# Reordering the seams of a two-layer hybrid attention block: the merge starts with its own loads, one projection moves ahead of the compressed keys, and the memory norm's transposes are emitted later

## The chip, the cores and the metric

The kernel runs on one core of one Trainium2 chip. Times are microseconds (us) on the device, for one execution of the whole program; the time shown is the median of three runs.

## What is computed

Two layers of a block on 1024 tokens of width 1024, in float32, with a memory of 256 rows. Cut to what matters here:

```python
def hybrid_layer(x, mem, ...):
    h = rms_norm(x, g_pre)
    parts = jnp.split(h @ w_in, IN_SPLITS, axis=-1)
    y_a = chunked_gmlp(a_u, a_v, ...) * silu(a_z)                  # branch 0
    y_b = nsa_attention(b_q, b_kc, b_vc, ...) * silu(b_z)          # branch 1
    y_c = forgetting_attention(c_q, c_k, c_v, ...) * silu(c_z)     # branch 2
    y_m = memory_attention(m_q, mem, g_mem, ...) * silu(m_z)       # branch 3
    up = einsum('bsnw,nwd->bsnd', stack([y_a, y_b, y_c, y_m]), w_br)
    gates = sigmoid(einsum('bsd,dne->bsne', h, w_gate))
    out = einsum('bsnd,bsnd->bsd', gates, up) @ w_o
    return x + rms_norm(out, g_post)

def memory_attention(q, mem, g_mem, w_mem_kv):
    mk, mv = split(rms_norm(mem, g_mem) @ w_mem_kv, 2)             # keys and values of the memory
    ...
def nsa_attention(...):
    kcmp, vcmp = compress(kc, ...), compress(vc, ...)              # silu(blocks @ w1) @ w2
    ...
```

## The kernel before, in words

**Arithmetic.** Every float32 operand of a large product is split into a high part and a low part (`split`: ScalarE copies the high part, VectorE or GpSimd subtracts it), and each product is three matmuls (`mm3`, lines 251, 254 and 255): high x high, high x low, low x high. One projection of 128 columns over all 1024 tokens (`proj`, twice) is 48 matmuls of 128x512. Weights are loaded by `weight` (DMA, then ScalarE and GpSimd split them) into rings of 2 or 3 tiles.

**Order.** The kernel emits its instructions in program order, and a planner (`schedule_with_timeline_sim=True`) then orders them for each engine by emission order and by its own model of time, over the whole program: an instruction that is ready may be placed before earlier ones that are not. `hot()` gives what is emitted inside it precedence over everything outside. `pace`/`follow`/`mark` add orderings between matmuls: each score matmul of the attention is a mark, and a paced projection's matmul k is tied behind a mark that lies proportionally far along. `order_slots` at the end adds one more rule: the tiles of one pool are first written in program order, so the first write of a tile waits for the first write of the tile allocated before it in its pool. All DMAs of the program are issued from one queue, SP's.

**Pools that matter here.** `st` is a ring of eight 128x512 tiles for everything short-lived (projection results, loads of y, gate results). `pp` is a ring of twelve 128x512 score tiles, open from `gates` to the end of `attention`. `yh` (five tiles of 128x4x512) opens in `merge`, after `pp` is closed, over the same memory, and waits tile by tile for what lay there. While `early` is True (in `gates` and until `fox` begins), two of three tiles asked of `st` come from `pp` instead, and projections take banks of two PSUM pools.

**A layer.** `gates` computes the gmlp branch's inputs, values, and some merge gates. `attention` (line 1255) runs `cmp_proj` (rope and split of the compressed branch's inputs, stored to `kcd` and `vcd`), `fox` (which begins with `compress`, the products of `kcd`/`vcd` at line 897, then four pairs of heads), `nsa_proj`, four `mem_proj` (queries of the memory attention, each 48 matmuls and four stores to `mqd`), and `nsa` with the memory units. Projections that come later in the program serve as filler between the score products. After the units, `FILL` lists paced filler: gmlp parts, early gates and `gate_out` (silu of a z projection, times the attention's output `od`, stored to `y`). Its last item is y4, an early gate.

**The merge.** In `merge` (line 1277) the first thing is `gate_out(1, "bz", 3)`, the one gate that needs the last heads of the nsa branch: for each half c it asks for tiles z and oo, loads oo from `od` (line 1215), computes z (tanh at line 341, product at 342), multiplies on GpSimd (1217) and stores y (1218). Then `add_branch(n)` for n = 0, 2, 3, 1 loads that branch's y (`get_y`, line 1316: eight loads), splits it into yh and yl (lines 331 and 335) and, for eight column blocks e and two token halves c, multiplies by w_br (twelve matmuls), loads or computes the gate th (line 1325) and accumulates (line 1332 for n = 0). Branch 0's y is written by the gmlp parts and does not need the last heads. Then `out_proj(0)`, `mem_norm` of the next layer (hot), `out_proj(1)`, and the next layer's `mem_kv` and `prenorm`. `norm_t` (line 377) loads a tile, scales it and at once turns it by transposes on TensorE (line 396) and splits it. `out_proj(c)` is two products of 96 matmuls (line 301), q = 0 and 1, each closed by squares on ScalarE (line 1359).

Of the kernel before, what the change touches and what calls it, by code (L numbers as in the profile page):

```python
# [19 lines left out]
F32 = mybir.dt.float32  # L20
# [193 lines left out]
class Net:  # L214
# [159 lines left out]
        nc.gpsimd.tensor_tensor(r, ms, self.mhalf, op=OP.pow)  # L374
        return r

    def norm_t(self, src, g, n_t, put):

        nc = self.nc
        for i in range(n_t):  # L380
            x = self.pvv.tile([128, 1024], F32, name="x", tag="slot")
            nc.sync.dma_start(x, src[i * 128:(i + 1) * 128, :])
            if i == 0:
                gb = self.ptp.tile([128, 2, 512], F32, name="gb", tag="pt2")
                nc.sync.dma_start(gb, g.rearrange("(q c) -> q c", q=2).partition_broadcast(128))
            r = self.rstd(x, EPS, i % 2 == 1)
            for q in range(2):
                xq = x[:, q * 512:q * 512 + 512]
                if q:
                    nc.scalar.activation(xq, xq, AF.Copy, scale=r)  # L390
                    nc.gpsimd.tensor_mul(xq, xq, gb[:, q])
                else:
                    nc.vector.scalar_tensor_tensor(xq, xq, r, gb[:, q], op0=OP.mult, op1=OP.mult)
                pt = self.ppt.tile([128, 4, 128], F32, name="pt")
                for k in range(4):
                    nc.tensor.transpose(pt[:, k, :], xq[:, k * 128:(k + 1) * 128], self.ident)
                hi, lo = put(i, q)
                self.split(hi, lo, pt)


    def layer(self, l):
# [709 lines left out]
            nc.sync.dma_start(self.y[0][g, :, cs], u)  # L1111


    def mem_norm(self, l):
        a = self.a
        mt = [[self.pkk.tile([128, 4, 256], R32, name="mt", tag="slot") for _ in range(2)] for _ in range(2)]
        def put(i, q):
            s = (slice(None), slice(None), slice(i * 128, i * 128 + 128))
            return mt[0][q][s], mt[1][q][s]
        with self.hot():  # L1120
            self.norm_t(a["mem"], a["g_mem"][l], 2, put)
        self.mt = mt

    def mem_kv(self):

        nc, mt = self.nc, self.mt
        m = lambda y, k: mt[y][k // 4][:, k % 4, :]
        for h in range(4):
            hi, lo = self.a_form(f"mk{h}")
            ps = self.pj()  # L1130
            self.mm3(ps[:, :256], [(hi[:, k, :], lo[:, k, :], m(0, k), m(1, k)) for k in range(8)])
            t = self.st("mk", R32)
            with self.hot():
                self.split(t[:, :256], t[:, 256:], ps[:, :256])
            self.move(self.mkd[h], t)
        for n in range(2):
            hi, lo = self.b_form(f"mv{n}")
            for i in range(2):
                ps = self.pj()
                sl = slice(i * 128, i * 128 + 128)  # L1140
                self.mm3(ps[:, :256], [(m(0, k)[:, sl], m(1, k)[:, sl], hi(k), lo(k)) for k in range(8)])
                t = self.st("mv", R32)
                with self.hot():
                    self.split(t[:, :256], t[:, 256:], ps[:, :256])
                for x in range(2):
                    v = t.rearrange("p (y h d) -> p y h d", y=2, h=2)[:, :, x, :]
                    self.move(self.mvd[2 * n + x, :, i], v)
# [60 lines left out]
    def gate_out(self, n, name, p):  # L1208
# [3 lines left out]
        for c in range(2):  # L1212
# [4 lines left out]
            nc.gpsimd.tensor_mul(z, z, o)  # L1217
            nc.sync.dma_start(self.y[n][p, :, cs], z)

    def gate_early(self, n, e):  # L1220

        w = self.a_form(f"g{n}{e}")
        for c in range(2):
            t = self.st("th")
            self.gate_store(n, e, c, t, self.proj(w, c))
# [28 lines left out]

    def attention(self):
        self.cmp_proj()
        self.fox()
        self.nsa_proj()
        for h in range(4):
            self.mem_proj(h)  # L1260
        self.todo = [(7 * h + 3 + 3 * c, lambda h=h, c=c: self.mem_unit(h, c)) for h in range(4) for c in range(2)]
        self.step, self.marks = 0, []
        self.nsa()
        names = FILL.split()
        self.pace = (0, sum(4 if n[0] == "u" else 2 for n in names) * 24 // (3 * STEP), STEP, SLACK)
        for name in names:
            h = int(name[1])
            if name[0] == "u":
                self.gmlp_u(h)
            elif name[0] in "wy":  # L1270
                self.gate_early({"w": 0, "y": 2}[name[0]], h)
            else:
                self.gate_out(*{"c": (2, "cz"), "m": (3, "mz"), "b": (1, "bz")}[name[0]], h)
        self.pace = None


    def merge(self):
        nc, tc, a, l = self.nc, self.tc, self.a, self.l
        p = lambda n, b: tc.tile_pool(name=n, bufs=b, reuse_waits="tile")
        with p("yh", 5) as self.pyh:  # L1280
            with p("acc", 1) as pacc:
                self.acc = [pacc.tile([128, 8, 512], F32, name=f"acc{c}") for c in range(2)]
                self.gate_out(1, "bz", 3)
                for n in (0, 2, 3, 1):
                    self.add_branch(n)
            gp = self.pyh.tile([128, 1024], F32, name="gp", tag="yh")
            nc.sync.dma_start(gp, a["g_post"][l].partition_broadcast(128))
            self.early = "banks"
            with p("kf", 4) as self.pkk, p("vf", 3) as self.pvv, p("tf", 1) as self.ptp:
                self.out_proj(0, gp)  # L1290
                if l + 1 < self.depth:
                    self.mem_norm(l + 1)
                self.out_proj(1, gp)
                if l + 1 < self.depth:
                    self.l, self.xsrc = l + 1, self.x1
                    self.fresh()
                    self.mem_kv()
                    self.prenorm()

    def add_branch(self, n):  # L1300
        yy = [self.get_y(n, c) for c in range(2)]
        for cs in ((0, 1),) if n != 1 else ((0,), (1,)):
            for e in range(8):
                wg = None if (n, e, 0) in self.ready else self.a_form(f"g{n}{e}")
                if e % 2 == 0:
                    wu = [z.rearrange("p (e w c) -> p e w c", e=2, w=4) for z in self.weight(f"u{n}{e // 2}")]
                for c in cs:
                    self.gated(n, e, c, wg, [z[:, e % 2] for z in wu], yy[c])
# [35 lines left out]
                for x in self.fin.pop(c):  # L1344
                    self.split(*x)

    def out_proj(self, c, gp):

        nc = self.nc
        hi, lo = self.mh[c]  # L1350
        ot = [self.pyh.tile([128, 2, 1024], F32, name="ot", tag="yh") for _ in range(2)]
        ss = [self.psm.tile([128, 2], F32, name="oss") for _ in range(4)]
        for q in range(2):
            qs = slice(q * 512, q * 512 + 512)
            def done(i, ps):
                sq = self.pcs.tile([128, 512], F32, name="sq", tag=("co", "si")[i % 2])
                with self.hot():
                    nc.vector.tensor_mul(ot[i // 2][:, i % 2, qs], ps, gp[:, qs])
                    nc.scalar.activation(sq, ps, AF.Square, accum_out=ss[i][:, q:q + 1])
            self.proj_wide(f"wo{q}", hi, lo, done, tail=c == q == 1)  # L1360
        for i in range(4):
            t0 = c * 512 + i * 128
            ms = self.psm.tile([128, 1], F32, name="oms")
            r = self.psm.tile([128, 1], F32, name="ors")
            with self.hot():
                nc.vector.reduce_sum(ms, ss[i], axis=AX.X)
                nc.vector.tensor_scalar(ms, ms, 1.0 / D, 4 * EPS, op0=OP.mult, op1=OP.add)
                nc.gpsimd.tensor_tensor(r, ms, self.mhalf, op=OP.pow)
            for x in range(2):
                xs = slice(x * 512, x * 512 + 512)  # L1370
                xr = self.st("xr")
                nc.sync.dma_start(xr, self.xsrc[t0:t0 + 128, xs])
                with self.hot():
                    nc.vector.scalar_tensor_tensor(xr, ot[i // 2][:, i % 2, xs], r, xr, op0=OP.mult, op1=OP.add)
                    nc.sync.dma_start(self.xdst[t0:t0 + 128, xs], xr)
# [87 lines left out]
```

## Time and profile before

| | us |
|---|---|
| median of 3 runs | 3156.19 (3148.03 to 3160.84) |
| the profiled execution's own time | 3157.73 |
| its span, first to last instruction | 3155.9 |
| TensorE busy | 3047.0 (97%) |
| VectorE, ScalarE, GpSimd busy | 1884.3, 1487.9, 1439.2 |
| mean granted TensorE clock | 0.989 of full |

A busy TensorE is one with a matmul under way; the idle time in brackets behind a row of the timeline is the time in which that engine stood still just before, and the name behind the arrow is what ended it. Layer 0 runs from 0 to about 1500, layer 1 from there to the end.

### The profile page before, as it was taken

Reading aid. Unit: us, or ns where it says so; the run is one execution under the profiler, and the core shown is the slowest. Engines: PE = TensorE matmul, PEld = TensorE weight load, DVE = VectorE, ACT = ScalarE, POOL = GpSimd, SP = SyncE. Lnnn points to the kernel's source line nnn. Section 1 sums busy time; section 2 is a strip of 40 time slices with the busy share of each in tenths; the row PEclk is TensorE's granted clock in tenths of the full one; section 3 lists DMA queues with packets and bytes.
Section 4 is the critical chain, followed back from the end, with each engine's and each line's share of the span. In section 5 each row is a group of like instructions: output and inputs, shape, how many; then the busy total and the mean of one; then the engine's idle time right before and its main releaser. Section 6 shows DMA issues by size and latency. Waiting matters only on the chain.

```text
span 3155.9 us, 45143 instructions
## 1 busy us (share of the span) xinstructions
PE 3047.0 (97%) x15168; PEld 2548.8 (81%) x15168; DVE 1884.3 (60%) x4313; ACT 1487.9 (47%) x3313; POOL 1439.2 (46%) x1142
## 2 busy tenths in 40 slices
PE   7999999999999999899999999999999999998998
PEld 6778878888888888688787788788878888886887
DVE  7555447868667855336474653578785678553363
ACT  5433345566556654323353433455655566552132
POOL 6844534543233322258577445355432333232684
PEclk9999999999999999999999999999999999998999
DMA  6544495564234322456665345855632342324564
GB/s 221 153 134 132 140 276 158 177 191 125 84 108 146 106 94 94 139 174 195 205 201 177 104 130 162 251 164 180 200 104 83 113 146 96 105 89 149 171 197 147
DMA packets 251673, 475.15 MB, mean 151 GB/s; under 512 B 42513, under 2 KB 96785, under 8 KB 251441
## 3 DMA queue, kind: packets, MB, share of 16 engines
q1 hardware_dynamic: 251440, 472.26, 47.6%
q8 instruction: 120, 1.97, 0.3%
q14 instruction: 113, 0.92, 0.1%
HBM read 334.73 MB, written 137.43 MB: 150 GB/s over the span
## 4 chain that ended last, share of the span: by engine, by line
PE 82%; DVE 5%; DMA 4%; POOL 3%; issue 2%; ACT 2%; SPq 1%; DVEq 0%; POOLq 0%; ACTq 0%
PE pj L251 11%; PE pj L254 11%; PE pj L255 11%; PE s L481 5%; PE s L301 5%; PE s L254 5%; PE o L645 5%; PE s L251 5%; PE s L255 5%; PE pt L633 5%; PE pj L481 4%; PE pj L301 4%; PE s L601 3%; PE s L602 3%; DVE p L674 1%
## 5 line engine op out<-in xcount | busy, mean ns | idle before, releaser
L229 POOL TENSOR_TENSOR wl<-wr,wh 128x1024 fp32r<-128x1024 f32 (+1 forms) x232 | 527.4, 2275 | 609.9 <-ACT wh L227 535.0
L251 PE MATMUL pj<-hh,wh 128*128 128x512 f32 x1648 | 651.5, 395 | 2.4 <-DVE z L342 1.8
L255 PE MATMUL pj<-hh,wl 128*128 128x512 f32 x1648 | 652.3, 396 | 0.0
L254 PE MATMUL pj<-hl,wh 128*128 128x512 f32 x1648 | 650.5, 395 | 0.0
L227 ACT ACTIVATE wh<-wr 128x1024 fp32r<-128x1024 f32 x232 | 245.5, 1058 | 341.1 <-PE s L254 86.7
L611 ACT ACTIVATE p<-p,nm 128x384 f32<-128x384 f32 (+3 forms) x512 | 306.8, 601 | 203.5 <-DVE nm L606 200.4
L333 DVE TENSOR_TENSOR pt<-pt,pt 128x512 fp32r<-128x512 f32 (+1 forms) x464 | 291.9, 635 | 134.8 <-ACT pt L331 133.4
L251 PEld LDWEIGHTS pj<-hh,wh 128*128 128x128 f32 x1648 | 310.9, 189 | 61.0 <-DVE z L342 2.7
L255 PEld LDWEIGHTS pj<-hh,wl 128*128 128x128 f32 x1648 | 310.6, 188 | 59.2
L254 PEld LDWEIGHTS pj<-hl,wh 128*128 128x128 f32 x1648 | 310.6, 188 | 58.0
L331 ACT ACTIVATE pt<-pt 128x512 fp32r<-128x512 f32 (+1 forms) x464 | 251.7, 554 | 212.5 <-PE pt L633 154.3
L645 PE MATMUL o<-pt,v 128*128 128x512 f32 (+1 forms) x864 | 245.1, 371 | 8.8 <-DVE pt L333 8.5
L654 POOL TENSOR_TENSOR yt<-yt 128x256 f32<-128x256 f32 x128 | 100.1, 782 | 300.9 <-ACT yt L653 241.0
L633 PE MATMUL pt<-ident,p 128*128 128x128 f32 x1488 | 230.6, 272 | 0.7 <-DVE pt L333 0.5
L251 PE MATMUL s<-yh,wh 128*128 128x512 f32 x512 | 201.1, 396 | 24.7 <-ACT yh L331 24.7
L633 PEld LDWEIGHTS pt<-ident,p 128*128 128x128 f32 x1488 | 184.9, 140 | 43.0 <-DVE pt L333 0.7
L254 PE MATMUL s<-yl,wh 128*128 128x512 f32 x512 | 201.4, 393 | 0.8 <-DVE yl L335 0.8
L255 PE MATMUL s<-yh,wl 128*128 128x512 f32 x512 | 200.7, 392 | 0.0
L601 PE MATMUL s<-kd,q 128*128 128x512 f32 (+2 forms) x512 | 187.4, 369 | 13.2 <-DVE nm L606 13.2
L602 PE MATMUL s<-kl,q 128*128 128x512 f32 (+2 forms) x512 | 175.5, 344 | 0.0
L645 PEld LDWEIGHTS o<-pt,v 128*128 128x128 f32 x864 | 147.6, 188 | 33.4 <-DVE pt L333 13.6
L676 DVE TENSOR_SCALAR p<-p,r,sg 128x384 f32<-128x384 f32 (+2 forms) x320 | 165.9, 574 | 1.7
(379 smaller groups left out, 6577.4 us busy)
## 6 DMA issues: line engine op xcount, KB each, us to landing
wr<-wt SPq DMA_DIRECT2D x250, 512.0 KB
th<-thd SPq DMA_DIRECT2D x124, 256.0 KB
thd<-gu SPq DMA_DIRECT2D x72, 256.0 KB
q<-rq SPq DMA_DIRECT2D x32, 512.0 KB
yf<-y SPq DMA_DIRECT2D x64, 256.0 KB
thd<-th SPq DMA_DIRECT2D x52, 256.0 KB
vd<-vs SPq DMA_DIRECT2D x48, 256.0 KB
v<-vd SPq DMA_DIRECT2D x24, 512.0 KB
```

What stands on the lines that cost most here:

```text
L229: nc.gpsimd.tensor_sub(lo[:, :n], raw[:, :n], hi.bitcast(F32)[:, :n])
L251: ins = nc.tensor.matmul(out, ah, bh, start=k == 0, stop=False)
L254: nc.tensor.matmul(out, ah, bl, start=False, stop=False)
L255: nc.tensor.matmul(out, al, bh, start=False, stop=k == n - 1)
L301: self.nc.tensor.matmul(ps[i], a[:, kk, ts], b[:, k], start=kk == n == 0, stop=kk == 7 and n == 2)
L333: (nc.gpsimd if pool else nc.vector).tensor_sub(lo, src, hi.bitcast(F32))
L481: nc.tensor.matmul(out, w[a][:, k], t[b][:, k], start=start and k == x == 0, stop=k == 3 and x == 2, skip_group_check=True)
L601: self.mark(nc.tensor.matmul(ps[:, :w], q[:, tq], kd[:, b0:b0 + w], start=True, stop=False), 1 + n / 128)
L602: nc.tensor.matmul(ps[:, :w], q[:, tq], kl[:, b0:b0 + w], start=False, stop=True)
L611: nc.scalar.activation(p[:, :n], p[:, :n], AF.Exp, bias=init, scale=-1.0, accum_out=l[:, x:x + 1])
L633: nc.tensor.transpose(pt[:, off + x * 128:off + x * 128 + 128], src, self.ident)
L645: nc.tensor.matmul(o[:, :, t0:t0 + m], it["v"], w[:, :, off:off + m], start=first, stop=last)
```

## The change

Three edits. (1) The merge no longer begins with `gate_out(1, "bz", 3)`. `add_branch(0)` asks for its eight loads of y first, then begins the gate (`gate_begin`: both projections and both silus, the matmuls tied behind the last score product), and finishes it (`gate_end`: loads of oo, multiplications, stores of y) when column block e = 2 comes up. (2) `mem_proj(0)` is emitted between `cmp_proj` and `fox`, so ahead of `compress`, while `early` is still True. (3) `mem_norm` of the next layer returns its transposes and splits unmade, and `out_proj(1)` emits them, hot, after its first product.

```diff
-    def norm_t(self, src, g, n_t, put):
+    def norm_t(self, src, g, n_t, put, later=False):
+        nc, rest = self.nc, []
+        def turn(xq, i, q):
+            pt = self.ppt.tile([128, 4, 128], F32, name="pt")
+            for k in range(4):
+                nc.tensor.transpose(pt[:, k, :], xq[:, k * 128:(k + 1) * 128], self.ident)
+            hi, lo = put(i, q)
+            self.split(hi, lo, pt)
...
-                pt = self.ppt.tile([128, 4, 128], F32, name="pt")
-                for k in range(4):
-                    nc.tensor.transpose(pt[:, k, :], xq[:, k * 128:(k + 1) * 128], self.ident)
-                hi, lo = put(i, q)
-                self.split(hi, lo, pt)
+                rest.append((xq, i, q))
+                if not later:
+                    turn(*rest.pop())
+        def all_rest():
+            for x in rest:
+                turn(*x)
+        return all_rest
...
+    def gate_begin(self, name, p):
+        w = self.a_form(f"{name}{p}")
+        zz = []
+        for c in range(2):
+            z = self.st("z")
+            self.silu2(z, self.proj(w, c))
+            zz.append(z)
+        return zz
+
+    def gate_end(self, n, p, zz):
+        for c, z in enumerate(zz):
+            cs = slice(c * 512, c * 512 + 512)
+            o = self.st("oo")
+            self.nc.sync.dma_start(o, self.od[n][p, :, cs])
+            self.nc.gpsimd.tensor_mul(z, z, o)
+            self.nc.sync.dma_start(self.y[n][p, :, cs], z)
...
     def attention(self):
         self.cmp_proj()
+        self.mem_proj(0)
         self.fox()
         self.nsa_proj()
-        for h in range(4):
+        for h in range(1, 4):
             self.mem_proj(h)
...
-                self.gate_out(1, "bz", 3)
                 for n in (0, 2, 3, 1):
                     self.add_branch(n)
...
                 self.out_proj(0, gp)
-                if l + 1 < self.depth:
-                    self.mem_norm(l + 1)
-                self.out_proj(1, gp)
+                rest = self.mem_norm(l + 1, True) if l + 1 < self.depth else None
+                self.out_proj(1, gp, rest)
...
     def add_branch(self, n):
         yy = [self.get_y(n, c) for c in range(2)]
+        if n == 0:
+            self.pace = (1, 1, 1, 0.0)
+            gated = self.gate_begin("bz", 3)
+            self.pace = None
         for cs in ((0, 1),) if n != 1 else ((0,), (1,)):
             for e in range(8):
+                if n == 0 and e == 2:
+                    self.gate_end(1, 3, gated)
...
-    def out_proj(self, c, gp):
+    def out_proj(self, c, gp, among=None):
...
             self.proj_wide(f"wo{q}", hi, lo, done, tail=c == q == 1)
+            if among and q == 0:
+                with self.hot():
+                    among()
```

## Rows read from the trace of the kernel before

**Rows 1.** The page: busy time of each engine; chain that ended last, by engine.

```profile
PE 3047.0 (97%) x15168; PEld 2548.8 (81%) x15168; DVE 1884.3 (60%) x4313; ACT 1487.9 (47%) x3313; POOL 1439.2 (46%) x1142
PE 82%; DVE 5%; DMA 4%; POOL 3%; issue 2%; ACT 2%; SPq 1%; DVEq 0%; POOLq 0%; ACTq 0%
```

**Rows 2.** Waits of PE, longest first in total: us, times, longest.

```profile
PE s L251 <- ACT yh L331: 24.7, 2, 12.6
...
PE pt L396 <- issue: 10.0, 4, 4.3
...
PE s L897 <- DMA cst<-kcd: 5.1, 4, 2.5
```

**Rows 3.** Timeline of PE, end of attention and start of merge: start, us, [idle before].

```profile
1262.86 0.42 PE L601 MATMUL s<-kd,q 128*128 128x384 f32 x1
...
1287.63 0.49 PE L633 MATMUL pt<-ident,p 128*128 128x128 f32 x3
...
1289.29 0.62 PE L645 MATMUL o<-pt,v 128*128 128x256 f32 x2 [0.58 <-DVE pt L333]
1302.02 0.79 PE L251 MATMUL s<-yh,wh 128*128 128x512 f32 x1 [12.11 <-ACT yh L331]
...
2871.85 0.80 PE L251 MATMUL s<-yh,wh 128*128 128x512 f32 x1 [12.61 <-ACT yh L331]
```

**Rows 4.** Timeline of the other engines and SP's queue across the same seam.

```profile
1265.74 0.57 ACT L518 ACTIVATE th<-pj 128x512 f32<-128x512 f32 x1
...
1266.34 0.32 SPq L521 DMA_DIRECT2D thd<-th  x1
...
1285.96 7.16 SPq L657 DMA_DIRECT2D o<-yt  x2
...
1288.68 0.56 DVE L333 TENSOR_TENSOR pt<-pt,pt 128x384 fp32r<-128x384 f32 x1 [0.76 <-ACT pt L331]
...
1294.64 0.33 SPq L1215 DMA_DIRECT2D oo<-o  x1
1297.36 0.60 ACT L341 ACTIVATE z<-pj 128x512 f32<-128x512 f32 x1 [5.51 <-DMA oo<-o]
1297.98 2.22 SPq L1316 DMA_DIRECT2D yf<-y  x5
...
1301.34 2.62 ACT L331 ACTIVATE yh<-yf 128x512 fp32r<-128x512 f32 x4 [3.38 <-DMA yf<-y]
1302.00 1.37 DVE L335 SCALAR_TENSOR_TENSOR yl<-yf,yh 128x512 fp32r<-128x512 f32 x2 [3.27 <-ACT yh L331]
```

**Rows 5.** Busy time by stretch, with its header.

```profile
core 0: us, PE busy (x) PEld busy (x) DVE busy (x) ACT busy (x) POOL busy (x), PEclk, DMA share, GB/s
...
1278.00:1290.00 12.00, 9.47 (x52) 6.61 (x50) 6.33 (x10) 7.08 (x14) 5.53 (x5) 1.00 0.23 71
...
1302.00:1307.60 5.60, 5.58 (x12) 4.08 (x13) 4.10 (x7) 3.81 (x7) 0.00 (x0) 0.50 1.01 348
1307.60:1313.20 5.60, 5.60 (x26) 4.63 (x25) 2.63 (x4) 0.60 (x1) 0.00 (x0) 1.00 1.00 349
...
2871.80:2877.80 6.00, 5.95 (x13) 4.42 (x14) 4.44 (x7) 4.11 (x7) 0.00 (x0) 0.50 1.02 350
```

**Rows 6.** Timeline of PE: the compressed products of both layers.

```profile
426.34 1.05 PE L897 MATMUL s<-cst,w 128*128 128x256 f32 x7 [1.52 <-DMA cst<-kcd]
...
1993.50 1.71 PE L897 MATMUL s<-cst,w 128*128 128x256 f32 x7 [2.48 <-DMA cst<-kcd]
```

**Rows 7.** Busy time by stretch: fox's end, where the projections have run out.

```profile
700.00:740.00 40.00, 36.61 (x200) 29.93 (x198) 36.11 (x90) 29.05 (x101) 18.34 (x17) 1.00 0.49 155
```

**Rows 8.** Layer 1's memory norm: timeline, and busy time of one stretch.

```profile
1501.71 0.33 SPq L382 DMA_DIRECT2D x<-mem  x1
...
1508.73 0.84 PE L396 MATMUL pt<-ident,x 128*128 128x128 f32 x4 [2.83 <-issue]
...
1539.69 0.60 ACT L1359 ACTIVATE sq<-s 128x512 f32<-128x512 f32 x1 [0.67 <-DVE oms L1366]
...
1505.90:1512.60 6.70, 3.88 (x15) 3.25 (x15) 2.65 (x7) 2.59 (x4) 3.37 (x3) 0.75 0.65 253
```

More of the change, by code (lines that the diff above doesn't have):

```diff
@@ L375, in rstd @@
         return r
-    def norm_t(self, src, g, n_t, put):
-        nc = self.nc
+    def norm_t(self, src, g, n_t, put, later=False):
[6 more added lines that the diff above has]
+            self.split(hi, lo, pt)
         for i in range(n_t):
@@ L1111, in gmlp_u, with mem_norm @@
             nc.sync.dma_start(self.y[0][g, :, cs], u)
-    def mem_norm(self, l):
+    def mem_norm(self, l, later=False):
         a = self.a
@@ L1120, in mem_norm @@
         with self.hot():
-            self.norm_t(a["mem"], a["g_mem"][l], 2, put)
+            rest = self.norm_t(a["mem"], a["g_mem"][l], 2, put, later)
         self.mt = mt
+        return rest
     def mem_kv(self):
```

## The prediction, made before the changed kernel was run

> **What bounds the kernel now.** I read the page first: TensorE is busy 97% of the span and carries 82% of the chain that ended last [rows 1]. The change adds and removes no matmul, so it can only move TensorE's idle time, some 109 us (span 3155.9 less 3047.0), and the time it runs at half clock. The list of TensorE's waits says where that lies [rows 2]: 24.7 us in two waits for the split of y, 10.0 for the transposes of line 396 (four waits, most of them in the first 30 us of the program, which no edit touches), 5.1 for the compressed keys' loads. Then the timelines of the three seams. At the merge of layer 0 the last product of the attention is over at 1289.9 and the next matmul starts at 1302.02, after 12.11 idle; in layer 1 it is 12.61 [rows 3]. The other engines show the chain behind it [rows 4]: the last heads' store (the second of the two issues of L657, at 1285.96 + 7.16 - 0.45 = 1292.67), the load of oo at 1294.64, the tanh of z at 1297.36, the loads of y from 1297.98, the split at 1301.34. Why z waits for oo and y waits for z is in the kernel's rule: tiles of `st` are first written in program order, and oo, z, oo, z stand before the eight tiles of y. Nothing in y of branch 0 needs the last heads. After the gap TensorE runs at clock 0.50: 12 matmuls in 5.6 us, where the next 5.6 us hold 26 [rows 5].
>
> **Edit 1, the merge.** Removed from the chain: store, load of oo, tanh, load of y. The eight loads now stand behind the two tiles of y4, whose last tanh is at 1265.74 and whose last store is issued at 1266.34 [rows 4]; I expect the loads there, more than 20 us before they are needed. The gate's 48 matmuls stay where they are: they run between the last score product at 1262.86 [rows 3] and about 1279 already, and the new tie to the last mark asks for no more. So TensorE should reach the last product at 1289.9 as before, and the question is when yh and yl may be written. They lie over score tiles. I count the allocations of `pp`: 122 in `gates` before, 125 with the three that the moved `mem_proj(0)` takes there, then 282 in the attention; the last unit's six tiles are the last six, ring places 5 to 10 of 12 after the change. yh of the first half covers places 0 to 3, which the unit before has left; yl covers 4 to 7 and waits for the last transposes, over at 1287.63 + 0.49 = 1288.1 [rows 3]. VectorE is then busy with the attention's last split until 1288.68 + 0.56 = 1289.24, and one piece of yl takes 1.37 / 2 = 0.69 [rows 4], so the first is there at 1289.9, when TensorE comes free; each further piece (0.69) is needed every three matmuls (3 x 5.6 / 26 = 0.65 [rows 5]). The silu of z slips two VectorE pieces in between. I put the idle time left at 1.0 per layer. Its lower end is 0. Its upper end: yh waits until everything under it is gone, the last store of the heads included (landed by 1294.64, when oo is issued), then 0.65 for a ScalarE piece (2.62 / 4) and 0.69 for a VectorE piece, 1296.0, so 6.1. I take the lower part because the pool waits tile by tile.
>
> Sum: idle 12.1 + 12.6 = 24.7; half clock: 12 matmuls in 5.6 instead of 12 x 5.6 / 26 = 2.6, 3.0 lost, and in layer 1 13 in 6.0 instead of 2.8, 3.2 [rows 5]; together 30.9, less 2 x 1.0: **28.9 gained**. With the upper ends (6.1 idle each and the clock down all the same): 24.7 - 12.2 = 12.5.
>
> Added: `gate_end`'s two loads, two GpSimd products and two stores. GpSimd has no work in the first stretches of the merge (0.00 busy twice [rows 5]), and y of branch 1 is needed only after branches 2 and 3: nothing. If that cover were gone it would be the old chain of two DMAs, some 5 us. The z tiles hold two of eight `st` places for about four gate blocks; the loads of th then run six ahead instead of eight, at 12 x 5.6 / 26 = 2.6 us each still 15 us of lead: nothing.
>
> What the early loads may hold up: SP's queue stands 7.16 us on two stores of which the second waits for its data [rows 4], and all behind it stands too. The last of the eight loads needs the place of y4's last tile, free when its store has landed, 1294.64 - 1292.67 = 1.97 after issue by the heads' store. Behind it are the stores of the last two units and weight loads, which have more slack than that: nothing. The Trainium skill says the same of any wait (DMA: Bandwidth & Descriptors, "Anatomy of one DMA": a semaphore wait is spent on the issuing sequencer, before dispatch). Taken as a charge against this change it would be 2.0 a layer and 3130 in place of 3126; the row agrees on the holding, and no row shows it reaching TensorE.
>
> **Edit 2, memory queries first.** The compressed products wait 5.1 in four waits [rows 2], 1.52 and 2.48 the largest [rows 6]. Ends: all of it goes, with a stretch at half clock up to 1.7 (6.8), or nothing. TensorE worked without a gap up to that wait on later projections, so it did not lack work; the planner put the products where its model had the loads landed, and it may do so again. I take half, 2.6. Against it: filler of 48 x 5.6 / 26 = 10.3 us a layer is spent before the units begin, and the stretch in which they run without filler grows by as much. There TensorE idles 3.4 of 40 us [rows 7]: 2 x 10.3 x 0.085 = 1.8. Its four stores of 256 KB may also push the loads back, 1.05 MB at 348 GB/s [rows 5] = 3.0 a layer at worst; the projection that it displaces stores as much, so nothing. Net 0.8 gained, ends -6.8 and +7.8.
>
> **Edit 3, the transposes.** They wait 2.83, with a mean clock of 0.75 over 6.7 us behind it (half of the time at half clock, at most 1.7 lost) [rows 8]: 4.5 at most, once. But they ran at 1508.7 inside `out_proj(0)`, though emitted after all of it, whose last squares come at 1539.7 [rows 8]. Place in the program did not hold them, because they are hot; emitted one product later and still hot, I expect them at the same place. Value 0; ends 4.5 gained, and 1 lost if they crowd the next layer's start.
>
> **Sum.** 28.9 + 0.8 + 0 = 29.7. From the profiled execution's 3157.73: 3128.0. The median of the runs is 1.5 lower, so 3126.5; I say 3126, 0.95% faster.
>
> **The rivals.**
> *Everything helps*: edits 2 and 3 reach their good ends and the merge keeps no idle time: 30.9 + 6.8 + 4.5 = 42.2, 3114. For it: those waits are all on TensorE, and nothing else bounds. Against: the planner's freedom.
> *The wait moves to the score tiles*: yh waits until the heads' last store is down, the clock still falls: 12.5 + 0.8, 3143. For it: the memory is shared; against: tile-by-tile waits and the count above.
> *The clock stays low without the gap*: five short waits of 0.4 to 0.6 precede the seam. There the granted clock is 1.00 at 9.47 of 12 busy [rows 5], which speaks against it. It would leave the 6.2 of half clock in place, 3133. The Trainium skill has such a rule (TensorE: Matmul & The Clock Gate, "A second HAM failure mode": short idles between groups of matmuls let the clock swing); this case's row disagrees.
> *The change does not do what it says*: the planner brings the loads of y no earlier: 3156.
> *Slower*: the place is fox, the mechanism missing filler. The units begin 10.3 us later and their filler ends 10.3 earlier, so up to 20.6 a layer run uncovered. At the row's idle share (0.085) that is 3.5 for both layers; if it were all idle, 41.2, and 3156 - 28.9 + 41.2 = 3168. It decides from an idle share of 0.70 on (28.9 / 41.2).
>
> **How the numbers follow.** Forecast 0.56 (its own range 3119 to 3134); everything helps 0.10; the clock 0.08; the wait moves 0.11; nothing moves 0.06; slower 0.09. Range 3110 (the best case and the runs' spread below it) to 3146 (the wait that moves, with 3.0 for the stores): left out are the last two cases and little else. About 0.5% (16 us) is what a measurement of this kernel can tell from no change: faster are the first three cases, 0.74; same are "moves" (13 us) and "nothing", 0.17; slower 0.09.
>
> **What would show it.** After: the wait of line 251 for the split of y falls from 24.7 to about 2; the loads of y are issued near 1266, before the last heads' store; the clock is 1.00 over the first 12 matmuls of both merges; line 897 still waits 2 to 3 in all; line 396 still waits about 2.8 inside `out_proj(0)`. It is wrong if line 251 still waits over 5 a layer, if the units of fox show new idle time near 700, or if y's loads stand behind oo's.

## The result, and the profile after

Beside the kernel before on one chip, the changed kernel took 3119.83 us (median of 4 runs, 3116.59 to 3122.03) against 3158.52: ratio 0.9883, 95% interval 0.9868 to 0.9897. A second comparison, on the chip of the single edits below, gave 3120.55 against 3155.43: 0.9891 (0.9877 to 0.9904). So it is 1.1 to 1.2% faster, some 34 to 37 us by the ratios, where 29.7 were forecast. The profiled execution took 3122.03, its span 3120.0.

The page of the changed kernel, the two lines that answer [rows 1]:

```profile
PE 3039.5 (97%) x15168; PEld 2545.0 (82%) x15168; DVE 1868.4 (60%) x4313; ACT 1487.2 (48%) x3313; POOL 1441.1 (46%) x1142
PE 82%; DMA 6%; DVE 5%; POOL 3%; issue 2%; ACT 2%; SPq 0%; DVEq 0%; POOLq 0%; ACTq 0%
```

The same number of matmuls takes 7.5 us less of busy time (the mean granted clock is 0.994 for 0.989), and there is 28 us less idle time. TensorE's waits in the changed kernel, which answer [rows 2] (us in total, times, longest; lines have shifted: 396 is now 384, 897 is 906, 601 is 610, 633 is 642, 645 is 654, 653 is 662, 657 is 666, 1215 is 1245, 1316 is 1350, 1332 is 1366):

```profile
PE pt L384 <- issue: 9.1, 4, 3.2
...
PE pt L642 <- DVE pt L333: 7.8, 6, 1.6
PE s L610 <- DVE nm L615: 5.0, 2, 2.5
PE s L251 <- DVE acc L1366: 4.2, 2, 2.3
...
PE s L906 <- DMA cst<-kcd: 3.3, 4, 1.1
...
PE s L251 <- ACT yh L331: 1.0, 2, 0.5
```

The wait for yh fell from 24.7 to 1.0. A new one stands in the merge: line 251 waits twice for acc, the tile in which VectorE sums the gated products. And in the attention the waits have changed places: nm is the row maximum that VectorE takes of the scores, pt the transposed scores that it splits. The kernel before had these two, which [rows 2] leaves out:

```profile
PE s L601 <- DVE nm L606: 13.2, 10, 2.9
...
PE o L645 <- DVE pt L333: 8.5, 14, 1.3
```

TensorE at the merge's start in the changed kernel, against [rows 3]; first layer 0, then layer 1:

```profile
1287.50 0.50 PE L251 MATMUL s<-yh,wh 128*128 128x512 f32 x1 [0.48 <-ACT yh L331]
1298.42 0.50 PE L251 MATMUL s<-yh,wh 128*128 128x512 f32 x1 [1.91 <-DVE acc L1366]
...
2833.62 0.50 PE L251 MATMUL s<-yh,wh 128*128 128x512 f32 x1 [0.48 <-ACT yh L331]
2844.90 0.50 PE L251 MATMUL s<-yh,wh 128*128 128x512 f32 x1 [2.29 <-DVE acc L1366]
```

The gaps of 12.11 and 12.61 are 0.48 each; 11 us into the merge TensorE stops once more. The other engines there, against [rows 4]:

```profile
1265.69 3.78 SPq L1350 DMA_DIRECT2D yf<-y  x8
...
1286.44 0.49 ACT L331 ACTIVATE pt<-pt 128x384 fp32r<-128x384 f32 x1 [0.94 <-PE pt L642]
1286.82 2.18 ACT L331 ACTIVATE yh<-yf 128x512 fp32r<-128x512 f32 x4
1288.90 0.59 ACT L341 ACTIVATE z<-pj 128x512 f32<-128x512 f32 x1
1289.38 0.60 ACT L662 ACTIVATE yt<-o 128x512 f32<-128x512 f32 x1
1289.86 2.21 ACT L331 ACTIVATE yh<-yf 128x512 fp32r<-128x512 f32 x4
...
1292.57 0.42 ACT L664 ACTIVATE yt<-yt 64x256 f32<-64x256 f32 x1
...
1292.57 1.28 SPq L1359 DMA_DIRECT2D th<-thd  x3
1293.94 0.45 SPq L666 DMA_DIRECT2D o<-yt  x1
...
1297.68 1.88 DVE L1366 SCALAR_TENSOR_TENSOR acc<-th,s 128x512 f32<-128x512 f32 x3 [3.87 <-DMA o<-yt]
```

y is loaded at 1265.69, before the last heads' store, as forecast. Read on: ScalarE now makes all eight pieces of yh around its two copies for the last heads (line 662, out of PSUM into yt, at 1289.38; line 664, from one half of yt to the other, at 1292.57), so their store is issued at 1293.94, 6.9 us after the attention's last product (which ends at 1287.01) and not 2.8 as before. VectorE's first sum waits 3.87 us for that store, because acc is laid over the yt tiles that this store reads (in layer 1 4.23, put down to the load of oo that stands behind that store; an experiment below moves acc and yt apart); meanwhile the PSUM tiles of the products fill up. Stretches of TensorE around it (us, busy with count, clock, DMA share, GB/s):

```profile
core 0: us, PE busy (x), PEclk, DMA share, GB/s
1287.50:1296.50 9.00, 9.00 (x38) 1.00 0.31 98
1299.60:1303.00 3.40, 3.40 (x10) 0.50 0.93 312
1303.00:1306.40 3.40, 3.40 (x16) 1.00 1.00 340
```

The first 38 matmuls run at the full clock, where before the first 12 ran at half [rows 5]. The half clock is not gone: it comes behind the wait for acc, in this profile in both layers. At the memory norm and at the compressed products little moved, against [rows 8] and [rows 6]:

```profile
423.91 1.10 PE L906 MATMUL s<-cst,w 128*128 128x256 f32 x7 [0.58 <-DMA cst<-kcd]
426.14 2.04 PE L906 MATMUL s<-cst,w 128*128 128x256 f32 x15 [1.12 <-DMA cst<-kcd]
...
1495.35 0.63 PE L384 MATMUL pt<-ident,x 128*128 128x128 f32 x4 [2.87 <-issue]
```

### The profile page after: what moved, and what is told of

Read it like the earlier page. It is cut to its first block, busy times and chain, and to the rows that moved or that the text cites. A ratio compares the mean times of both kernels' runs of the same rounds, so it can differ in the third digit from the quotient of the medians.

```text
span 3120.0 us, 45163 instructions
## 1 busy us (share of the span) xinstructions
PE 3039.5 (97%) x15168; PEld 2545.0 (82%) x15168; DVE 1868.4 (60%) x4313; ACT 1487.2 (48%) x3313; POOL 1441.1 (46%) x1142
## 4 chain that ended last, share of the span: by engine, by line
PE 82%; DMA 6%; DVE 5%; POOL 3%; issue 2%; ACT 2%; SPq 0%; DVEq 0%; POOLq 0%; ACTq 0%
PE pj L251 11%; PE pj L255 11%; PE pj L254 11%; PE s L490 5%; PE s L301 5%; PE o L654 5%; PE pt L642 5%; PE s L254 4%; PE s L251 4%; PE s L255 4%; PE pj L490 4%; PE pj L301 4%; PE s L610 3%; PE s L611 3%; DMA wr<-wt 2%
## 5 line engine op out<-in xcount | busy, mean ns | idle before, releaser
L251 PE MATMUL pj<-hh,wh 128*128 128x512 f32 x1632 | 644.5, 395 | 4.5 <-DVE rd L807 2.5
L255 PE MATMUL pj<-hh,wl 128*128 128x512 f32 x1632 | 643.2, 394 | 0.0
L1369 POOL TENSOR_TENSOR acc<-acc,th 128x512 f32<-128x512 f32 x96 | 131.8, 1382 | 66.4 <-DVE th L1368 59.0
```

The lines of the kernel that those rows point to most:

```text
L251: ins = nc.tensor.matmul(out, ah, bh, start=k == 0, stop=False)
L255: nc.tensor.matmul(out, al, bh, start=False, stop=k == n - 1)
```

## The experiments

Two theories. A: edit 1 carries some 20 us or more, held down by the wait for acc; edit 2 carries the rest; edit 3 nothing. B: edit 1 carries it all, and what other stages gained is chance. First the three edits one by one, and the changed kernel beside them.

**Edit 1 alone.** Into the kernel before: `gate_begin` and `gate_end`, and

```diff
-                self.gate_out(1, "bz", 3)
...
+        if n == 0:
+            self.pace = (1, 1, 1, 0.0)
+            gated = self.gate_begin("bz", 3)
+            self.pace = None
...
+                if n == 0 and e == 2:
+                    self.gate_end(1, 3, gated)
```

> The kernel before with edit 1 alone (the merge begins with y's loads, the last gate is held back); the compressed products and the memory norm as before. Theory A (edit 1 carries a part, the rest is edit 2): the two gaps at the seam shrink from 24.7 to about 1 us and the sum's wait for its third block, 4.2 us in two with its half clock, comes in, so about 20 to 22 us less than before (ratio 0.993). Rival B (edit 1 carries everything, and what the other stages gained was chance of single profiles): 33 to 37 us less, ratio 0.988 to 0.9895. What the prediction said of this edit: 28.9 less, ratio 0.991. Every theory expects line 251 on ACT's yh at 1 to 2 us in all and the wait for acc (DVE) at 4 to 5 us.

3128.5 (6 runs) against 3155.43: 0.992 (0.9903 to 0.9937), 25 us less (20 to 31). The wait for acc is there, 4.7 in two. B, which wants the whole gain, is out; the forecast's 28.9 and A's 20 to 22 both lie in the interval, and the time does not choose between them.

**Edit 2 alone.**

```diff
         self.cmp_proj()
+        self.mem_proj(0)
         self.fox()
...
-        for h in range(4):
+        for h in range(1, 4):
```

> The kernel before with edit 2 alone (the memory queries of head 0 ahead of the compressed products). Theory A: 8 to 15 us less than before (ratio 0.995 to 0.9975): the stages that shrank in the changed kernel outside the merge (line of the compressed product 6.7 us earlier in layer 1, its attention 4.4 us shorter) shrink here too. Rival B: within 3 us of before, ratio 0.999 to 1.001, with the wait of the compressed products for kcd going from 5.1 to about 3.3 us. The prediction said 0.8 less. The seam into the merge stays as before: 24.7 us in two gaps.

3148.05 (7 runs): 0.9973 (0.9963 to 0.9983), 8.5 us less (5 to 12). A's size holds. Of its two stages layer 1's attention is shorter (861.9 for 865.7), the stretch between `out_proj(0)` and the compressed products less so than A has it (500.4 for 502.5). The wait for kcd, which B wants shorter, is 5.4, as long as before. What changed is the waits in the attention: those on nm are 4.8 in two for 13.2 in ten, and line 633's on pt have come in, 7.8 in six for 0.5 in two.

**Edit 3 alone**: `norm_t`, `mem_norm` and `out_proj` as in the diff, nothing else.

> The kernel before with edit 3 alone (the memory norm's transposes later in the program). Both theories: no change, ratio 0.999 to 1.001, since the transposes keep their place in TensorE's order; the wait of 2.8 us ahead of them stays inside out_proj(0). Rival C (edit 3 carries part of the gain): 4 us less or more, with the transposes behind the second product's start and no low clock at that place. Its spread also tells how far two kernels with one order of work differ.

3154.52 (11 runs): 0.9997 (0.9989 to 1.0006). No change.

**The changed kernel again.**

> The changed kernel once more, beside the three parts on one chip: 37 us less than before, ratio 0.987 to 0.990. Theory A: the three single edits' gains add up to it within 4 us. Rival B: edit 1 alone comes to it within 4 us. If the profile of this run shows the stages outside the merge (layer 1 up to its compressed products, 6.7 us; its attention, 4.4 us) as long as before while the median stays, the gain there was the single profile's.

3120.55: 34.9 below; the three parts give 26.9 + 7.4 + 0.9 = 35.2 by their medians. They add up, and B is out. Of the two stages outside the merge layer 1's attention is short again (861.2), but the stretch up to its compressed products takes 500.6, against 494.2 in the first profile and 502.5 before: most of that gain was the single profile's.

**Where the wait for acc comes from.** In the changed kernel only the order of the pools is changed, so that acc lies over other tiles:

```diff
-                    p("yt", 3) as self.pyt, p("kk", nb["kk"]) as self.pkk, \
-                    p("vv", nb["vv"]) as self.pvv, p("tp", 2) as self.ptp:
+                    p("kk", nb["kk"]) as self.pkk, \
+                    p("vv", nb["vv"]) as self.pvv, p("tp", 2) as self.ptp, p("yt", 3) as self.pyt:
```

> The changed kernel with the heads' copy-out buffers (yt) laid out last in their block, so that the sum (acc) no longer lies over them; the rest as in the changed kernel. Theory A (the merge's fourth block of matmuls waits because acc's first sum waits for the last heads' store out of yt): the wait of line 251 on DVE's acc, 4.2 us in two, and the half clock behind it (1.7 each) go, 4 to 8 us less than the changed kernel: ratio to before 0.9865 against 0.989. Rival B (the sum is late for another reason, the th loads behind the stores on SP): the wait stays at 4 us and the time with it, 0.988 to 0.990.

3114.84: 0.9867 (0.985 to 0.9885), 5 to 6 us below the changed kernel by the medians of runs on different chips, with intervals that overlap; the rows decide. The wait for acc is gone from the list. The store is issued just as late (1290.52, 6.95 us after the attention's last product), but VectorE's first sums now wait for th instead, and earlier:

```profile
1291.97 0.69 DVE L1366 SCALAR_TENSOR_TENSOR acc<-th,s 128x512 f32<-128x512 f32 x1 [1.58 <-DMA th<-thd]
1293.84 1.28 DVE L1366 SCALAR_TENSOR_TENSOR acc<-th,s 128x512 f32<-128x512 f32 x2 [1.18 <-DMA th<-thd]
```

The seam, from the attention's last product to `out_proj(0)`, layer 0 and then layer 1 (us, busy with count, clock, DMA share, GB/s), in three kernels: before, changed, changed with yt last.

```profile
1289.91:1491.01 201.10, 188.37 (x818) 0.97 0.57 181
2859.24:3060.51 201.27, 188.45 (x818) 0.96 0.56 181
```

```profile
1287.01:1477.58 190.57, 187.95 (x819) 0.99 0.58 183
2833.14:3024.62 191.48, 188.08 (x818) 0.99 0.57 182
```

```profile
1283.57:1470.18 186.61, 186.06 (x820) 1.00 0.58 187
2829.78:3017.47 187.69, 186.36 (x819) 1.00 0.58 186
```

Both layers together take 402.4, 382.1 and 374.3. Then the same move of yt on the kernel before, with edit 1 and by itself:

> The kernel before with edit 1 alone and yt laid out last, so that the first sums don't wait for the last heads' store. Theory A (of edit 1's forecast, 28.9 us, only the slot of acc was mis-costed): the seam (from the end of attention's last product to out_proj, both layers) falls by 27 to 28 us, as in the changed kernel with yt last, and the time by 28 to 33: ratio 0.9895 to 0.991. Rival B (most of what yt's place gained lay elsewhere): as edit 1 alone, 0.992, with the wait for acc gone.

> The kernel before with yt laid out last and nothing else. Theory A (yt's place matters only where the merge starts before the last heads' store has landed): no change, 0.999 to 1.001, and both gaps of 12 us still there. Rival B (the layout itself gains, in attention or in DMA traffic): 4 to 6 us less, 0.998.

With edit 1: 3125.49, 0.9907 (0.9894 to 0.9921), and no wait for acc; its seam:

```profile
1287.09:1473.90 186.81, 186.09 (x818) 1.00 0.58 187
2835.65:3022.57 186.92, 186.07 (x819) 1.00 0.59 187
```

373.7, 28.6 less than before. The time alone does not tell this kernel from edit 1 without the move (0.992); the rows do, 373.7 against 383.1. By itself the place of yt does nothing: 1.0004 (0.9995 to 1.0013). A holds in all three, the seam a little beyond its 27 to 28.

**The gate not held back.** In the changed kernel:

```diff
-            gated = self.gate_begin("bz", 3)
+            self.gate_end(1, 3, self.gate_begin("bz", 3))
```

> The changed kernel with the last gate not held back: its loads of oo, products and stores of y are issued as soon as the gate's projections are, ahead of the first blocks of the merge. Theory A: SP then stands at the load of oo until the last heads' store has landed, ahead of the th loads that the first sums read, so the sums come later: the wait for acc grows from 4.2 to 5 to 9 us, 1 to 5 us more than the changed kernel, ratio to before 0.989 to 0.991. Rival B (holding back is worth nothing, since the th loads wait for the same store): within 1 us of the changed kernel.

3128.19: 0.9912 (0.9898 to 0.9925), 7.6 above the changed kernel by the medians (another chip; by the ratios 7 to 9); A's direction, and more than it said. The wait for acc is 8.7, within A's 5 to 9. SP's queue and VectorE's first sum show why:

```profile
1290.69 0.33 SPq L1245 DMA_DIRECT2D oo<-o  x1
1291.96 0.45 SPq L666 DMA_DIRECT2D o<-yt  x1
1294.04 0.33 SPq L1245 DMA_DIRECT2D oo<-o  x1
1294.46 0.38 SPq L1357 DMA_DIRECT2D th<-thd  x1
...
1298.27 0.69 DVE L1364 SCALAR_TENSOR_TENSOR acc<-th,s 128x512 f32<-128x512 f32 x1 [6.33 <-DMA th<-thd]
```

The loads of th stand behind the second oo, which waits for the heads' store; in the changed kernel three of them go ahead of that store (1292.57). So the holding back, which the forecast took as free, is worth 5 to 7 us at the seam (386.9 against 382.1 and 380.3).

**Why edit 2 gains.** Two heads' queries ahead of the compressed products, and one head's queries still further ahead, before `cmp_proj`, where they no longer stand between the stores of kcd and their use (in both the loop over the heads begins at the first one left, as in edit 2; cut here):

```diff
         self.cmp_proj()
+        self.mem_proj(0)
+        self.mem_proj(1)
         self.fox()
...
```

```diff
+        self.mem_proj(0)
         self.cmp_proj()
         self.fox()
...
```

> The kernel before with edit 2 for two heads (memory queries of heads 0 and 1 ahead of the compressed products), edits 1 and 3 not made. Theory A (edit 2 gains because the cover moved ahead fills the waits of the compressed products, as its 48 matmuls stand between loads and use): little beyond one head, 7 to 11 us less than before, and the wait for kcd falls below 3 us. Rival B (edit 2 gains because the order of the filler matmuls in the first stage of attention changes, and the waits there and the low clock behind them with it; the wait for kcd was not shortened by one head, 5.4 against 5.1 us): the kcd wait stays at 4 to 7 us, and the time goes by where the waits on nm and pt come out, anywhere from 15 less to 10 more. Rival C (the missing filler of the first stage, named in the prediction): 6 to 12 us more than before, with idle time between 430 and 750 us.

> The kernel before with head 0's memory queries still earlier, ahead of the compressed branch's own projections instead of behind them, so that they don't stand between its loads and its products; the filler that is taken from the rest of the attention is the same as in edit 2. Theory A (the cover in front of the compressed products gains): the gain of edit 2, 8.5 us, is gone, 0.999 to 1.001. Rival B (the filler's new order later in the attention gains): 6 to 11 us less than before again, with two waits on nm instead of ten and the wait for kcd at 5 to 7 us.

Two heads: 3144.78, 0.9964 (0.9951 to 0.9977), 11 us less; the wait for kcd is 3.4, between what A and B said, and C is out. Ahead of `cmp_proj`: 3165.7, 1.0032 (1.002 to 1.0045), 10 us slower than before, with the wait for kcd down to 3.3. Both theories missed on the second: the cover at the compressed products does not set the time, since the wait there was as short in the slowest kernel as in the changed one's first profile (3.3 each), and moving the queries forward is no gain by itself either. What goes with the time is the attention's idle time (from the first compressed product to the last product, both layers). Before, edit 2, and queries ahead of `cmp_proj`:

```profile
426.34:1289.91 863.57, 850.43 (x4493) 1.00 0.43 135
1993.50:2859.24 865.74, 852.74 (x4493) 0.99 0.43 135
```

```profile
422.90:1287.47 864.57, 852.89 (x4505) 0.99 0.45 136
1988.71:2850.64 861.93, 850.12 (x4505) 1.00 0.45 136
```

```profile
437.08:1295.54 858.46, 841.82 (x4445) 0.99 0.43 134
2008.60:2867.30 858.70, 840.36 (x4445) 1.00 0.44 134
```

Idle: 13.1 + 13.0 = 26.1, then 11.7 + 11.8 = 23.5, then 16.6 + 18.3 = 35.0. The counts show in what the slow kernel differs: it has 48 matmuls a layer less in the stage than the kernel before. With edit 2 the moved queries take the place of other filler ahead of the compressed products (in layer 0, 1880 matmuls run before the first of them, 1891 in the kernel before); ahead of `cmp_proj` they come on top of it (1940). So the filler left to the attention is not, as expected, the same as in edit 2. The slow kernel waits more for pt in line 645 (15.7 in 22, for 8.5 in 14 before), and has waits near 700, and at the same place in layer 1, that no other kernel has, for ScalarE's copy of the heads out of PSUM:

```profile
698.50 0.73 PE L645 MATMUL o<-pt,v 128*128 128x512 f32 x2 [2.10 <-ACT yt L653]
...
2269.53 0.99 PE L645 MATMUL o<-pt,v 128*128 128x512 f32 x2 [2.98 <-ACT yt L653]
```

**Edit 3 made real**: the changed kernel, the transposes no longer `hot`.

```diff
             if among and q == 0:
-                with self.hot():
-                    among()
+                among()
```

> The changed kernel with the memory norm's transposes not marked urgent, so that they really come behind the first half of out_proj(1) in TensorE's order. Theory A (in the changed kernel edit 3 moves nothing, so the wait ahead of the transposes, 2.8 to 3.7 us, is still paid inside out_proj(0); moved for real it goes): 2 to 5 us less than the changed kernel, ratio to before 0.9865 to 0.9885. Rival B (the transposes' results are then late for the memory keys, or the scratch they write comes free late): within 1 us of the changed kernel or up to 3 more.

3117.48: 0.9884 (0.987 to 0.9897), not told apart from the changed kernel's 0.9891. In the rows the transposes do move: between 1470 and 1620 line 384 no longer waits on issue or for x (in the changed kernel's two profiles 4.0 and 5.4 us there). The stretch from `out_proj(0)` to the memory's keys, 409 matmuls, is 5.2 us shorter than in the changed kernel's second profile, shown below it (there 3.8 idle and one low stretch, here 0.4 idle and none), and 2.8 shorter than in its first (93.4, with 3.1 idle and no low stretch):

```profile
1475.44:1566.09 90.65, 90.21 (x409) 1.00 0.63 208
```

```profile
1470.98:1566.84 95.86, 92.07 (x409) 0.98 0.59 197
```

**What gained, together**: the changed kernel with yt last and two heads' queries ahead.

> The changed kernel with yt laid out last and the memory queries of two heads, not one, ahead of the compressed products: the two that gained put together. If they add up: 5 us less than the changed kernel for yt and 2.5 less for the second head, 3111 to 3114 us, ratio 0.9855 to 0.9870. If the order of the filler comes out otherwise with edit 1 in place, between 0.985 and 0.990.

3109.77, the lowest median of all; 0.9864 (0.9849 to 0.988), far below the kernel before and 10 us below the changed kernel's medians, with intervals that overlap. From the changed kernel with yt last (0.9867) it can't be told apart.

All profiles side by side. "Low" counts the stretches of 3.4 us at clock 0.50 inside the attention; in each the work of 1.7 us at the full clock is lost. Seam, idle and low are each of one profiled execution.

| kernel | ratio | seam us | attention idle us | low |
|---|---|---|---|---|
| before | 1 | 402.4 | 26.1 | 6 |
| edit 3 | 0.9997 | 401.8 | 27.5 | 5 |
| yt last | 1.0004 | 402.0 | 27.7 | 7 |
| edit 1 | 0.9920 | 383.1 | 24.5 | 8 |
| edit 1, yt last | 0.9907 | 373.7 | 24.4 | 3 |
| edit 2 | 0.9973 | 401.8 | 23.5 | 4 |
| two heads | 0.9964 | 401.5 | 21.1 | 3 |
| ahead of `cmp_proj` | 1.0032 | 401.8 | 35.0 | 5 |
| changed (twice) | 0.9883, 0.9891 | 382.1, 380.3 | 24.1, 23.2 | 3, 2 |
| not held back | 0.9912 | 386.9 | 22.7 | 2 |
| not hot | 0.9884 | 379.1 | 23.9 | 1 |
| changed, yt last | 0.9867 | 374.3 | 23.5 | 2 |
| changed, yt last, two heads | 0.9864 | 373.3 | 18.8 | 2 |

## Why the prediction was right, and where it was not

**The time**: 3126 was said, within 3110 to 3146, faster; 3119.8 came. The forecast's mechanism at the merge held. Two terms of the sum were mis-sized, in opposite directions: the seam gave 7 to 9 us less than said, edit 2 some 7 to 8 more. That the sum came as close as it did is in part luck.

**Edit 1, the term "idle time left, 1.0 per layer", and the half clock taken as gone.** Up to there it came nearly as written: loads near 1266, 0.48 idle, full clock over the first matmuls of both layers, and no new wait of TensorE for a load in edit 1's list. The 0.48 is a wait for the first piece of yh, which ScalarE makes behind its last split of the attention, and not for VectorE's yl, of which the prediction worked out its figure. But the prediction asked only of yh and yl what lies under them. acc lies over yt, and the last heads' copies into yt, and so their store, come later than before because ScalarE now splits y first. That left 1.91 and 2.29 us more idle, with one stretch at half clock behind each; in the second profile 2.16 and 2.19, with such a stretch in layer 1 alone. Line 251 waits 5.2 us in all (1.0 for yh, 4.2 for acc) where about 2 was said. The seam gained 20.3 and 22.1 us in the two profiles, not 28.9. With acc's wait taken away it gained 28.1 and 28.6: the rest of the term was right within 0.8 us, though by two small misses that cancel (with edit 1 and yt last 24.0 of idle and 4.7 of busy time, where 22.7 and 6.2 were forecast). The rival "the wait moves to the score tiles" named the right release (the last heads' store) for the wrong tile.

**The cost of `gate_end`: nothing.** Right because it is held back; issued at once it cost 5 to 7 us at the seam. The Trainium skill's rule that speaks against this change (DMA: Bandwidth & Descriptors, "Anatomy of one DMA": a semaphore wait is spent on the issuing sequencer) bore on this place and not on y's loads: SP's rows of that experiment agree with it, the loads of th going out only behind the waiting oo.

**Edit 2: "0.8 gained".** Wrong as a sum: 8.5 (5 to 12) came. Half of the compressed products' wait, 2.6, was to go; it stayed in the single edit (5.4 for 5.1) and went in part in the changed kernel (3.3 and 4.8 in its two profiles). And the prediction priced the filler only where it runs out, 700 to 740, and as a loss. That stretch lost nothing, against [rows 7]:

```profile
700.00:740.00 40.00, 37.63 (x206) 1.00 0.58 185
```

The gain lies over the whole attention. The five kernels that leave the queries where they were idle there 24.4 to 27.7 (mean 26.0) with 3 to 8 low stretches (mean 5.8); the six with one head's queries behind `cmp_proj`, the second profile of the changed kernel counted, idle 22.7 to 24.1 (23.5) with 1 to 4 (2.3). That is 2.5 + 3.5 x 1.7 = 8.5 us. It is an account by means of few profiles: without edit 1's profile, a slow one (see below), it is 2.9 + 2.9 x 1.7 = 7.8, and the single edit's own profile gives 2.6 + 2 x 1.7 = 6.0. Which of the planner's choices makes one order of filler better than another was not settled: one head and two behind `cmp_proj` gave 8.5 and 11 less, one head ahead of it 10 more.

**The slower rival** (filler missing in fox) did not come with the change, since edit 2 leaves as many matmuls to the attention as before (4503 to 4505 for 4493 a layer). The queries ahead of `cmp_proj` show it: 48 matmuls a layer less for the attention, idle time near 700 among the rest, 8.9 us more idle in both layers, between the rival's 3.5 and 41.2, and a time 10 above before.

**Edit 3: 0.** Right, and for the reason given: still hot, the transposes keep their place (17.8 us into the stage for 17.7) and their wait (2.87 for 2.83). Its good end, 4.5, lies between the 2.8 and the 5.2 by which the stretch is shorter when they really move; the time could not confirm it. (Of the four waits of [rows 2] two, 5.6 of the 10.0 us, lie at the program's start: most of the time, not most of the waits.)

**"The clock stays low without the gap"**: no. Ahead of the seam stand the same short waits (0.37 to 0.48), and the clock over the merge's first 38 matmuls is 1.00. The Trainium skill's rule (TensorE: Matmul & The Clock Gate, "A second HAM failure mode") does not show itself there; the clock falls behind the single waits of 1.91 and 2.29.

**Not placed**: of the changed kernel's two profiles the seam explains 20.3 and 22.1 us, the attention 2.0 + 3 x 1.7 = 7.1 and 2.9 + 4 x 1.7 = 9.7 (table, against before), so 27.4 and 31.8 of the 35.9 and 36.8 by which their spans are shorter. The 8.5 and 5.0 us left are not placed; two profiles of the changed kernel itself differ by 6.4 us in one of the stages between (494.2 and 500.6, above). The profiled run of edit 1 alone, 3143.76, was the slowest of its six and has five low stretches ahead of its first compressed product, where the others have one or two, so its stages can't be set against its median.

## What to carry to other kernels

When a stage is pulled forward, ask of every tile that it writes, the sums as well as the inputs, what lies under it and who empties that; then ask what the engine that empties it has been given to do first. Work that runs as filler is priced over the whole stretch in which it fills, not only where it runs out: count what is left in that stretch after the move. And an order that a planner makes must be measured: three ways of moving the same kind of queries spread over 21 us.

## What the runs showed of the hardware

The granted clock does not fall behind every wait of the same length. Behind the transposes' wait it fell to 0.50 in the kernel before (2.83 us, [rows 8]) and stayed at 1.00 in the first profile of the changed kernel (2.87). At one place of one kernel it did both: at the merge of layer 0 it fell behind 1.91 us in the first profile of the changed kernel and stayed at 1.00, from 1292 to 1305, behind this wait in the second:

```profile
1293.18 0.50 PE L251 MATMUL s<-yh,wh 128*128 128x512 f32 x1 [2.16 <-DVE acc L1366]
```

So whether a single wait of some 2 us costs such a stretch (1.7 us) could not be told ahead here. Over the whole attention the stretches weighed more than the idle time itself (3.5 of them, 6.0 us, against 2.5 us idle, by the means above).
